# Closing a gated-unit kernel with one barrier: GpSimd waits for the landings between gather and release

## Chip, cores, metric

One core of a Trainium2 chip. The metric is the device time of one execution in microseconds (us). Three runs of the kernel before, taken first, gave a median of 936.13 us (935.86 to 936.99). The program uses one core, so its runs are compared run by run; all runs here are of the fast state, with a granted clock of 1.0.

## The reference

```python
def reference(x):                       # x: 8192 x 8192 float32
    a, b = np.split(x, 2, axis=-1)
    return a * (1 / (1 + np.exp(-b)))   # 8192 x 4096
```

## The kernel before

32 tiles of 128 partitions; each partition holds two rows. SyncE issues loads, ScalarE takes the sigmoid, VectorE multiplies, ScalarE issues stores. The last tile is split in eight pieces, so that its stores start early.

```python
    for i in range(n_tiles):
        x_sb = pool.tile([P, R * n_cols], fp32)
        o_sb = pool.tile([P, R * half], fp32)
        load = nc.sync.dma_start(out=x_sb, in_=x_t[i])
        ...
        n = 4 if i == n_tiles - 1 else 1
        ...                                   # for each row and piece:
                nc.scalar.activation(out=b, in_=b, func=SIG)
                nc.vector.tensor_mul(out=o_sb[:, cols], in0=a, in1=b)
                if n > 1:
                    nc.scalar.dma_start(out=out_t[i, :, cols], in_=o_sb[:, cols])
        if n == 1:
            nc.scalar.dma_start(out=out_t[i], in_=o_sb)
```

The closing is not written in the kernel; the framework adds it as the program's third block. In order: SyncE waits for nine semaphores (eight of DMA lanes, which the transfers use in turn, and one of VectorE) ahead of a drain (an instruction that the traces call DRAIN; it can carry waits and updates of semaphores); barrier one, in which every other engine adds 1 to a gather semaphore and GpSimd, having seen 4, adds 4 to a release semaphore; GpSimd's reset drain and a clear of the kernel's semaphores; barrier two.

## Time and profile before

| | before |
|---|---|
| median of the first 3 runs | 936.13 us |
| span, first to last instruction (profiled run of 935.99 us) | 933.924 us |
| last landing (sixteenth increment of the last store's semaphore) | 933.047 us |
| tail: last landing to the end of the span | 0.877 us |

A store has landed when its semaphore has its sixteenth increment. The page, the queue waits and the closing instructions of this kernel are shown in the prediction. Times to the nanosecond are starts and semaphore updates as the trace records them. "From start to start" is the time from one instruction's start to that of the next one on the path; the durations that the views print are shorter, because waiting and propagation are not in them.

### The profile page before, as it was taken

What the parts mean: (1) busy time and instruction counts of PE and PEld (TensorE: products, weight loads), DVE (VectorE), ACT (ScalarE), POOL (GpSimd) and SP (SyncE); (2) the same over time, 40 slices, a digit from 0 to 9 for tenths busy, and PEclk for the clock granted to TensorE, in tenths of its full rate; (3) what the DMA queues carried; (4) which work ended last, traced back from release to release, by engine and by line L of the source; (5) the groups of instructions that cost most, each with busy time, mean ns of one, the idle gap of its engine ahead of it and who ended that gap; (6) DMA issues with size and microseconds to landing.
All of it is one profiled execution on the core that took longest, in us unless ns stands there. A gap on an engine that the chain in (4) does not pass through costs nothing.

```text
span 933.9 us, 410 instructions
## 1 busy us (share of the span) xinstructions
DVE 280.9 (30%) x70; ACT 230.0 (25%) x71; POOL 0.2 (0%) x4
## 2 busy tenths in 40 slices
DVE  0333321333213333133331333312333123331234
ACT  1313331133311333203332033320233202333023
POOL 0000000000000000000000000000000000000000
DMA  9999999999999999999999999999999999999998
GB/s 404 420 434 431 453 418 429 439 434 449 420 456 404 452 424 427 449 425 451 412 459 410 438 438 425 451 421 452 413 449 421 431 445 443 429 420 453 410 446 362
DMA packets 10226, 402.67 MB, mean 431 GB/s; under 512 B 1136, under 2 KB 1136, under 8 KB 2160
## 3 DMA queue, kind: packets, MB, share of 16 engines
q1 hardware_dynamic: 4608, 268.44, 66.5%
q10 hardware_dynamic: 5616, 134.22, 33.3%
q14 instruction: 2, 0.02, 0.0%
HBM read 268.44 MB, written 134.22 MB: 431 GB/s over the span
## 4 chain that ended last, share of the span: by engine, by line
DMA 78%; DVE 15%; ACT 6%; issue 0%; DVEq 0%; ACTq 0%
DMA x_sb<-in_x_dram 78%; DVE o_sb L39 15%; ACT x_sb L38 6%; DVEq L61 0%; ACTq L41 0%; ACTq L38 0%
## 5 line engine op out<-in xcount | busy, mean ns | idle before, releaser
L39 DVE TENSOR_TENSOR o_sb<-x_sb 128x4096 f32<-128x4096 f32 (+1 forms) x70 | 280.9, 4056 | 647.2 <-ACT x_sb L38 647.2
L38 ACT ACTIVATE x_sb<-x_sb 128x4096 f32<-128x4096 f32 (+1 forms) x70 | 228.7, 3315 | 695.9 <-DMA x_sb<-in_x_dram 691.8
L38 ACT ACT_TABLE_LOAD x1 | 1.3, 1283 | 0.8 <-PEq L85 0.8
L85 POOL MEMSET const-uint8-127<- 128x1 uint8 x1 | 0.1, 103 | 0.0
L85 POOL MEMSET const-bfloat16-1.0<- 128x1 bf16 x1 | 0.1, 102 | 0.0
L85 POOL MEMSET const-float32-0.0<- 128x1 f32 x1 | 0.1, 99 | 0.2 <-issue 0.2
L85 POOL MEMSET const-float32-1.0<- 128x1 f32 x1 | 0.1, 99 | 0.0
## 6 DMA issues: line engine op xcount, KB each, us to landing
out_dram<-o_sb ACTq DMA_DIRECT2D x31, 4096.0 KB, 41.7
out_dram<-o_sb ACTq DMA_DIRECT2D x8, 512.0 KB, 6.2
x_sb<-in_x_dram SPq DMA_DIRECT2D x32, 45.5
```

Of the source, the lines that this page charges most:

```text
L38: nc.scalar.activation(out=b, in_=b, func=SIG)
L39: nc.vector.tensor_mul(out=o_sb[:, cols], in0=a, in1=b)
L85: nc = _bacc.Bacc("TRN2", target_bir_lowering=False, num_devices=1)
```

## The change

The intent: all engines meet once instead of twice. SyncE no longer waits for stores; it arrives early. GpSimd gathers, waits for the landings itself, resets and clears, and then releases.

```diff
-        load = nc.sync.dma_start(out=x_sb, in_=x_t[i])
-        first = first or load
+        nc.sync.dma_start(out=x_sb, in_=x_t[i])
...
+def _launch_early(nc):            # first load ahead of the entry drain, as before
...
+def _one_closing_barrier(nc):
+    block = nc.main_func.blocks[2].instructions
+    waits = block[0]
...
+    drain1, gather1, release1, reset, clear, drain2, gather2, release2 = pool
+    others = [i for i in block[1:] if i.engine != POOL]
+    arrive_and_leave = others[: len(others) // 2]
+    last = stores[-1].sync_info.on_update[0].id
+    landings = sorted(waits.sync_info.on_wait, key=lambda w: w.id == last)
+    pool_waits = [
+        mybir.InstEventSemaphore(engine=POOL, ...on_wait=[w]...)
+        for w in landings
+    ]
+    block[:] = arrive_and_leave + [drain1, gather1, *pool_waits, reset, clear, drain2, release1]
```

More of the change, by code (lines that the diff above doesn't have):

```diff
@@ L22, in _tiles @@
     pool = ctx.enter_context(tc.tile_pool(name="io", bufs=2))
-    first = None
     for i in range(n_tiles):
@@ L43, in _tiles @@
             nc.scalar.dma_start(out=out_t[i], in_=o_sb)
-    return first
+def _launch_early(nc):
+    SP = mybir.EngineType.SP
+    entry, body = (b.instructions for b in nc.main_func.blocks[:2])
+    load = next(i for i in body if i.engine == SP and i.opcode == "DMACopy")
+    assert not load.sync_info.on_wait
+    body.remove(load)
+    where = next(k for k, i in enumerate(entry) if i.engine == SP and i.opcode == "Drain")
+    entry.insert(where, load)
+def _one_closing_barrier(nc):
+    SP, POOL = mybir.EngineType.SP, mybir.EngineType.Pool
+    block = nc.main_func.blocks[2].instructions
+    waits = block[0]
+    assert waits.engine == SP and waits.opcode == "Drain" and len(waits.sync_info.on_wait) > 1
+    pool = [i for i in block if i.engine == POOL]
+    drain1, gather1, release1, reset, clear, drain2, gather2, release2 = pool
+    assert reset.is_reset_sema and clear.opcode == "ISA"
+    others = [i for i in block[1:] if i.engine != POOL]
+    arrive_and_leave = others[: len(others) // 2]
+    stores = [i for i in nc.main_func.blocks[1].instructions if i.opcode == "DMACopy"]
+    last = stores[-1].sync_info.on_update[0].id
+    landings = sorted(waits.sync_info.on_wait, key=lambda w: w.id == last)
+    pool_waits = [
+        mybir.InstEventSemaphore(
+            name=nc.get_next_instruction_name(),
+            engine=POOL,
+            debug=waits.debug,
+            sync_info=mybir.SyncInfo(on_wait=[w], on_update=[]),
+        )
+        for w in landings
+    ]
+    block[:] = arrive_and_leave + [drain1, gather1, *pool_waits, reset, clear, drain2, release1]
 @with_exitstack
@@ L61 @@
     tc.compile()
-    blocks = nc.main_func.blocks
-    entry, body = blocks[0].instructions, blocks[1].instructions
-    SP = mybir.EngineType.SP
-    at = next(k for k, i in enumerate(body) if i.engine == SP)
-    load = body[at]
-    assert load.opcode == "DMACopy" and not load.sync_info.on_wait
-    del body[at]
-    where = next(k for k, i in enumerate(entry) if i.engine == SP and i.opcode == "Drain")
-    entry.insert(where, load)
+    _launch_early(nc)
+    _one_closing_barrier(nc)
 _INS = ['x']
```

## The prediction

> **What bounds the kernel now.** I read the page first, for the limit of the whole run, then the queue waits of SyncE, then narrow windows of the closing line (line 61, to which every closing instruction is booked), and last the semaphore records of the trace for times to the nanosecond. From the page:
>
> ```profile
> span 933.9 us, 410 instructions
> ...
> DVE 280.9 (30%) x70; ACT 230.0 (25%) x71; POOL 0.2 (0%) x4
> ...
> DMA  9999999999999999999999999999999999999998
> ...
> DMA packets 10226, 402.67 MB, mean 431 GB/s; under 512 B 1136, under 2 KB 1136, under 8 KB 2160
> ...
> DMA 78%; DVE 15%; ACT 6%; issue 0%; DVEq 0%; ACTq 0%
> ```
>
> The DMA row is full in every slice but the last; no engine is busy a third of the time. The 402.67 MB set the time. The change moves no byte and no compute instruction, so it can act only after the last transfer has landed. How long is that stretch? SyncE's queue waits name its beginning:
>
> ```profile
> SPq L61 <- DMA out_dram<-o_sb: 63.4, 3, 61.1
> SPq L61 <- PEq L61: 0.6, 2, 0.4
> ```
>
> The first line is SyncE waiting, at the end, for stores to land. The second is SyncE waiting in the barriers, 0.6 us in two waits; nothing of that can be gained beyond what lies after the landing. Windows of 0.25 us at the end (columns: window, its length, busy time of DVE, ACT and POOL, clock, DMA share, GB/s) show the transfers die out:
>
> ```profile
> 932.50:932.75 0.25, 0.00 (x0) 0.00 (x0) 0.00 (x0) 1.00 0.04 16
> 932.75:933.00 0.25, 0.00 (x0) 0.00 (x0) 0.00 (x0) 1.00 0.00 0
> ```
>
> The last packet ends at 932.721 us; the sixteenth increment of the last store's semaphore comes at 933.047. The span ends at 933.924. So everything the change can touch is 933.924 - 933.047 = 0.877 us, 0.09% of the time. GpSimd's closing instructions from 933.3 on (duration in ns, then first and last start):
>
> ```profile
> L61 POOLq EVENT_SEMAPHORE  x3: 17/17/17, 933.4 to 933.8; - x3
> L61 POOLq DRAIN  x2: 34/52/70, 933.4 to 933.7; - x2
> L61 POOLq EVENT_SEMAPHORE_RANGE_CLEAR  x1: 93/93/93, 933.5 to 933.5; - x1
> ```
>
> With the first gather at 933.282 these are: gather, release, reset drain, clear, drain, gather, release. The range clear really is short, 93 ns, so resetting the kernel's semaphores is a small cost; what takes time is the row of steps.
>
> **The 0.877 us, step by step**, each as the time from one start to the next (trace records, ns): landing to SyncE's wait for it, 16; to its next wait instruction (two other semaphores, long satisfied), 64; to the drain that carries the last wait, 68; to the drain that arrives at barrier one, 55; to GpSimd's gather, 32; to its release, 79; to its reset drain, 80; to the clear, 100; to the second drain, 121; to the second gather, 79; to the second release, 78; to the end of the last engine's leaving (TensorE, its 51 ns wait being the slowest), 105. Sum 877. The other engines re-arrive for barrier two by 933.587 us, before GpSimd gathers at 933.741, so the second barrier costs only GpSimd's own instructions.
>
> **What the Trainium skill says.** "Perfetto Trace Analysis", section "Sequencer-only Instruction (DRAIN, etc)": only the execution of such an instruction is reported, the wait before and the propagation after it are not. The trace agrees: the twelve instructions of the path have durations of 28, 28, 7, 7, 17, 17, 70, 93, 34, 17, 17 and 51 ns, 386 together, of 877 from start to start. I therefore count starts, not durations. "DMA: Bandwidth & Descriptors", section "Anatomy of one DMA — SWDGE (gpsimd) path": data move at bytes / 436e9, and the semaphore fires only when the last byte is confirmed in memory. Those transfers are of the software queue and ours of the hardware queues, yet the rate fits: 402.67 MB / 436 GB/s = 923.6 us of the span's 933.9; the confirmation here takes 933.047 - 932.721 = 0.33 us. Neither part is touched. "Runtime: NRT & Kernel Launch", section "The ~15µs preamble/postamble breakdown": a closing barrier of about 1.5 us, a semaphore reset of about 1.5 us and about 2 us of barrier and DMA re-arming follow the kernel. In this case only 935.99 - 933.92 = 2.07 us of the profiled run's time lies outside the span, so not all of that is in the metric; the measurement decides. The changed kernel leaves this part as it is.
>
> **The change part by part.**
> - *Moving the first load ahead of the entry drain* is in both kernels; the diff only rewrites how the load is found. The dropped return value does nothing. 0.
> - *SyncE no longer waits for the landings.* It arrives as soon as its last issue is done. Removed from the path: 16 + 64 + 68 + 55 ns, and the 32 ns from its arrival to the gather: 235 ns.
> - *Gather one moves ahead of the landing.* With SyncE early, the last to arrive is ScalarE, whose closing drain ends at 928.708 us; the gather falls near 928.74, over 4 us before the landing. Its 79 ns to the next instruction leave the path.
> - *GpSimd gets the waits, one semaphore each.* The old waits name nine semaphores in five instructions (four pairs and a single), so nine new instructions. At GpSimd's pace of some 79 ns that is 0.7 us, but the sort puts the last store's semaphore at the end. The store before it lands at 931.813 us, 1.234 us ahead of the last; all eight others are checked by then or at most 8 x 79 = 0.63 us after. One wait is left on the path: from the semaphore's update to GpSimd's start I take 23 ns (in the old gather: 933.259 to 933.282). Added: 23.
> - *Reset, clear and drain stay*, once: 80 from the wait to the reset drain (as from release one to it), 100, 121.
> - *Gather two goes*: 78 ns less. The drain is followed by the one release, 79 ns as a drain was followed by gather two, and the leaving takes 105.
>
> New tail: 23 + 80 + 100 + 121 + 79 + 105 = 508 ns. Removed 235 + 79 + 78 = 392, added 23: gain 369 ns. Check: 877 - 369 = 508. Time: 936.13 - 0.37 = 935.76 us.
>
> **Rivals.**
> - *The nine waits land on the path* (the last store's is not last, or other stores land after it). Then up to eight of 79 ns, 0.63 us, follow the landing and turn the gain into a loss of 0.26: 936.4 us. For it: one wait for each instruction where SyncE took two. Against: the sort, and landings in the order of issue, 1.2 to 1.3 us apart (929.316, 930.575, 931.813, 933.047).
> - *GpSimd is slower than SyncE to see a DMA's semaphore.* The trace has GpSimd waiting only for engines' updates; a poll of 0.1 to 0.2 us would leave 0.2 of gain: 935.9 us.
> - *The gain is hidden outside the span*: if the 2.07 us after and before it are paced by something else, 936.1 us. Against: the trace's first record after the program comes 0.235 us after the last engine leaves, as if it follows it.
> - *Chance.* Three runs of the same kernel range over 935.86 to 936.99, 1.13 us, three times the gain. This is the likeliest to decide the measured sign: a queue that lands a little later outweighs all of this. The result can read as slower without any step being wrong.
> - *More than expected*, because the old barrier disturbs the transfers: I see nothing for it; at the end no engine waits on them and the stretch is 0.09%.
>
> **Range and chances.** The centre is 935.76. The spread of a median of three I take from the old runs, which lie 0.27 under and 0.86 over their median, and make it a little wider for another session: 935.0 to 936.8. To be 2% faster the kernel would have to lose 18.7 us, where the whole tail is 0.877; 2% slower has no source either, only a disturbed run. Within 2%: 0.98.
>
> **What would show it right or wrong.** In the changed kernel's trace: SyncE has no wait for stores at the end; GpSimd's waits start about 928.8 us, all but one before the last landing; one gather and one release; the tail from the sixteenth increment to the span's end is 0.51 us against 0.88. A tail over 0.7 would mean waits on the path or a slow poll; I then look at which wait starts after the landing. If the tail is 0.51 and the time is not lower by 0.37, the transfers or the stretch outside the span took the difference. The landing time itself (933.05) should move only by chance; if it moves in every run by more than 1 us in one direction, my claim that the change acts only after the landing is wrong.

## The result, and the profile after

Six runs each: 935.98 us median after (935.07 to 936.74), 936.02 before (935.64 to 936.99). The ratio is 0.9998, 95% interval 0.9985 to 1.0011: the same. (A ratio is the mean time of one kernel's runs over the mean of the other's of the same rounds, so not quite the ratio of the medians quoted.) By time alone nothing can be said of a gain of 0.37 us.

The page after, with the same rows as before:

```profile
span 934.6 us, 399 instructions
...
DMA  9999999999999999999999999999999999999998
...
DMA packets 10226, 402.67 MB, mean 431 GB/s; under 512 B 1136, under 2 KB 1136, under 8 KB 2160
```

The transfers are the same; 11 instructions are gone. The profiled run is longer than that of before (span 934.628 against 933.924 us), yet its tail is shorter: its last landing is at 934.128 us, 1.08 us later than in the run of before, and the tail is 0.500 us in place of 0.877. SyncE's queue waits show the first part of the change:

```profile
SPq L97 <- PEq L97: 62.7, 1, 62.7
```

All closing instructions are now on line 97. SyncE has one wait there, for the barrier, and none for a store; before, it waited 63.4 us for stores. (The view infers who ended a wait, and names TensorE's queue, PEq. By the semaphore records it is GpSimd's release, at 934.548 us, that SyncE's instruction at 934.565 follows.) GpSimd's closing instructions (duration in ns as minimum, median, maximum, then first and last start in us) show the second part:

```profile
L97 POOLq EVENT_SEMAPHORE  x6: 17/42/43, 931.0 to 934.5; - x6
L97 POOLq DRAIN  x2: 34/52/70, 934.2 to 934.5; - x2
L97 POOLq EVENT_SEMAPHORE_RANGE_CLEAR  x1: 92/92/92, 934.3 to 934.3; - x1
```

Six event instructions: one gather (931.0, three microseconds ahead of the last landing), four waits and one release. The diff writes nine waits. The lowering (the step that makes the program's final instructions) folded them two to an instruction and put the one left over, VectorE's, on the reset drain. The same view cut to the time after the landing (934.13 on) shows what is left on the path:

```profile
L97 POOLq EVENT_SEMAPHORE  x2: 17/30/42, 934.2 to 934.5; - x2
L97 POOLq DRAIN  x2: 34/52/70, 934.2 to 934.5; - x2
...
L97 PEldq EVENT_SEMAPHORE  x1: 51/51/51, 934.6 to 934.6; - x1
```

GpSimd has one wait and one release left here. Before, SyncE had two event instructions and a drain with a wait after the landing, and GpSimd two gathers and two releases. From start to start, in ns:

| step | before | predicted | after |
|---|---|---|---|
| landing to the wait for it | 16 | 23 | 24 |
| SyncE: two more steps, arrival; gather; release | 64+68+55+32+79 | - | - |
| to the reset drain | 80 | 80 | 87 |
| to the clear | 100 | 100 | 99 |
| to the second drain | 121 | 121 | 122 |
| to gather two, to the release | 79+78 | 79 | 63 |
| to the last engine's leaving | 105 | 105 | 105 |
| sum | 877 | 508 | 500 |

### The profile page after: what moved, and what is told of

It reads as the page before. It is cut to its first block, busy times and chain, and to the rows that moved or that the text cites. A ratio compares the mean times of both kernels' runs of the same rounds, so it can differ in the third digit from the quotient of the medians.

```text
span 934.6 us, 399 instructions
## 1 busy us (share of the span) xinstructions
DVE 280.9 (30%) x70; ACT 230.0 (25%) x71; POOL 0.2 (0%) x4
## 4 chain that ended last, share of the span: by engine, by line
DMA 78%; DVE 15%; ACT 6%; issue 0%; DVEq 0%; ACTq 0%
DMA x_sb<-in_x_dram 78%; DVE o_sb L37 15%; ACT x_sb L36 6%; DVEq L97 0%; ACTq L39 0%; ACTq L36 0%
```

## The experiments

In the full kernel the time moves by 1 us from run to run, so most experiments use the kernel cut to its last tile. Its output is wrong: only the last 256 rows are written, and the rest stays as it was found. It takes some 40.5 us. Each tail is read from one trace, so it is that of a single execution. The first four cut kernels ran in one call on one chip, s_last_first, s_release_first and s_no_clear in a second on another, s_last_early in a third; the kernel before, timed in all three, had medians of 935.90, 935.91 and 935.93 us. The cut is this line, and the closing is varied on top of it:

```diff
-    for i in range(n_tiles):
+    for i in range(n_tiles - 1, n_tiles):
```

**The two ends.** The cut kernel with the closing of before, and with that of the change.

> The kernel before cut to its last tile (output wrong on purpose), closing as it was. Theory: the closing after the last landing is the same 0.88 us as in the full kernel (0.877), on a total of 50 to 65 us; run-to-run spread well under the full kernel's 1.1 us, say 0.2, because little is left to vary. Rival (the spread comes from the start or from what lies outside the span): the spread stays near 1 us.

> The changed kernel cut to its last tile (output wrong on purpose). Theory: tail 0.50 us from the sixteenth increment of the last store to the end, so the median is 0.38 us under that of the cut kernel before. Rival one, hidden outside the span: same median within 0.1. Rival two, the gain in time is larger than in the span (the full runs had 1.8 us outside the span against 2.07 in the one run of before that shows it): 0.5 to 0.7 us less.

Measured: tails of 0.791 and 0.499 us; medians of 40.76 us (40.73 to 40.80) and 40.57 us (40.44 to 40.80). In the profiled runs the time falls from 40.73 to 40.44, by as much as the tails; that is partly luck, since the last landing is also 0.047 us earlier (38.109 against 38.156). Over four runs each the medians differ by 0.19, half of the 0.38 expected. By these two alone the gain in device time isn't shown: s_after spreads over 0.36 us, which I had not expected of so short a kernel, and its slowest run is as slow as that of s_before (40.80). The cut kernel's old closing is 0.09 us shorter than the full kernel's, for a reason that SyncE's closing instructions in s_before show:

```profile
L97 SPq EVENT_SEMAPHORE  x6: 17/28/1278, 31.9 to 38.9; - x6
```

One of these waits is recorded with 1278 ns: the one that holds the last store's semaphore (landing at 38.156 us) and the one before it (36.883 us). It stands last in SyncE's row, so only the drain follows; in the full kernel another pair stood between. The record of this wait begins at 36.900 us, 17 ns after the first-named of its two semaphores, and ends just after the second-named. In these traces the order of the names counts, and not which of the two comes first: the three other pairs of SyncE in this trace also begin 17 ns after the first-named, whose second had landed 2.4 us or more before, and they are recorded with 28 ns.

**Half the change: one barrier, SyncE still waits.**

```diff
-    block[:] = arrive_and_leave + [drain1, gather1, *pool_waits, reset, clear, drain2, release1]
+    block[:] = [waits, *arrive_and_leave, drain1, gather1, reset, clear, drain2, release1]
```

> Half of the change, last tile only: one barrier, but SyncE still waits for the landings and arrives after them. Theory: tail 16+64+68+55+32 = 235 ns to the gather, then 80+99+122+63+105: 0.70 us, so 0.17 us less than the cut kernel before. Rival (the second barrier alone is what costs): tail 0.50, as in the changed kernel.

Measured: tail 0.620 us, 0.171 less than s_before; the expected saving of 0.17 is right (the level is lower by the 0.09 just told). Median 40.50 us (40.48 to 40.62), lower than s_after's 40.57 though the tail is 0.121 us longer: the times don't resolve this step. SyncE still holds the long wait, and GpSimd has one gather and one release:

```profile
L97 SPq EVENT_SEMAPHORE  x5: 17/28/1277, 31.8 to 38.6; - x5
L97 POOLq EVENT_SEMAPHORE  x2: 17/17/17, 38.2 to 38.6; - x2
```

**The other half: GpSimd waits, two barriers.**

```diff
-    block[:] = arrive_and_leave + [drain1, gather1, *pool_waits, reset, clear, drain2, release1]
+    arrive_again = others[len(others) // 2 :]
+    block[:] = arrive_and_leave + [drain1, gather1, *pool_waits, release1, reset, clear]
+    block[:] = list(block) + arrive_again + [drain2, gather2, release2]
```

> The other half, last tile only: GpSimd waits for the landings between gather and first release, and the second barrier stays. Theory: tail 24+87+80+99+122+79+78+105 = 0.67 us, 0.20 us less than the cut kernel before. The two halves' gains (0.17 and 0.20) then add up to the whole 0.38. Rival (the move of the waits gains nothing): tail 0.88.

Measured: tail 0.699 us, 0.092 less than s_before, not 0.20. Most of the miss is the shorter level of s_before (0.09 of 0.11); the rest is that the release, which now carries two of the waits, takes 106 ns to the reset drain and not 80. Median 40.58 us (40.55 to 40.73). SyncE waits only in the two barriers, GpSimd has eight event instructions:

```profile
L99 SPq EVENT_SEMAPHORE  x2: 17/17/17, 38.2 to 38.7; - x2
L99 POOLq EVENT_SEMAPHORE  x8: 17/30/43, 35.8 to 38.7; - x8
```

Both halves gain, 0.171 and 0.092 us, 0.263 together, and the whole 0.292. Of the 29 ns missing, 26 are these 106 ns in place of 80: the lowering places the waits differently in each program. The rival "only the second barrier costs" fell with s_one_sync (0.620 against 0.499), and "moving the waits gains nothing" with this run. This is said of the tails, by the traces.

**The order of the waits.** First the sort turned round.

```diff
-    landings = sorted(waits.sync_info.on_wait, key=lambda w: w.id == last)
+    landings = sorted(waits.sync_info.on_wait, key=lambda w: w.id != last)
```

> The changed kernel cut to its last tile, with the one sort key turned round: GpSimd checks the last store's semaphore first, so the others are checked after it has landed. Theory: the waits are folded in pairs, each step costs 87 ns, three to four more steps stand after the landing: tail 0.76 to 0.85 us, against 0.50. Rival (satisfied waits are free, only the last landing counts): tail 0.50 to 0.55.

I had the direction wrong. The tail is 0.412 us, shorter than s_after by 0.087; median 40.27 us (40.22 to 40.29). The trace shows why: the first wait of the list is the one that stays on the reset drain and is checked last, and the pairs are checked ahead of it. The drain starts 24 ns after the landing, and one step of 87 ns is gone. GpSimd's closing in s_last_first: the same six events and two drains as in the changed kernel, the first drain now starting at 38.1 us (landing 38.055, start 38.079):

```profile
L97 POOLq DRAIN  x2: 34/52/70, 38.1 to 38.3; - x2
```

So that run did not test what I meant it for. With the last store's semaphore put into the fifth place instead, the folding checks it first:

```diff
+    pool_waits[4], pool_waits[-1] = pool_waits[-1], pool_waits[4]
     block[:] = arrive_and_leave + [drain1, gather1, *pool_waits, reset, clear, drain2, release1]
```

> The cut changed kernel with the last store's semaphore swapped to the fifth place of the list, which the folding puts into the first pair that GpSimd checks; the other checks then stand after the landing. Theory: each pair costs 87 ns though it is satisfied, so the tail is 24 + 4 x 87 + 99+122+63+105 = 0.76 us, and the time is 0.26 us over the cut changed kernel's 40.5. Rival (satisfied waits are nearly free, only the landing counts): tail 0.50.

Measured: tail 0.728 us, median 40.66 us (40.63 to 40.76). GpSimd's events:

```profile
L98 POOLq EVENT_SEMAPHORE  x6: 17/43/2167, 36.0 to 38.8; - x6
```

The 2167 ns are the first pair, held until the last landing. After it come three pairs and the drain, from start to start 87, 86 and 87 ns, though all their semaphores had been met for over a microsecond. The first of them starts 79 ns after the landing, not 24 + 87 as I had reckoned; that is the 0.03 us under the expected 0.76. Satisfied waits are not free; the rival fell. This is the loss that the prediction's first rival was about (the waits land on the path): 0.23 us over s_after.

**Release ahead of the clear, and no clear at all.**

```diff
-    block[:] = arrive_and_leave + [drain1, gather1, *pool_waits, reset, clear, drain2, release1]
+    block[:] = arrive_and_leave + [drain1, gather1, *pool_waits, release1, reset, clear, drain2]   # s_release_first
+    block[:] = arrive_and_leave + [drain1, gather1, *pool_waits, release1]                         # s_no_clear
```

> The changed kernel cut to its last tile, with the release moved ahead of reset and clear: the other engines leave while GpSimd clears. Theory: tail 24+87+80+99+122+34 = 0.45 us, GpSimd now being the last to end, 0.05 us less than 0.50; hardly to be seen in the time. Rival (what follows starts from the other engines and not from GpSimd): the time falls by 0.25 us or more.

> The changed kernel cut to its last tile, without reset, clear and the drain after them. Theory: tail 24+87+105 = 0.22 us, so 0.28 us less than the cut changed kernel, in span and in time. Rival (the clear only moves to the end of the program, where the same work is done anyway): time within 0.1 of the cut changed kernel. It may also give a wrong result in later rounds if the semaphores are not at zero when it starts again.

s_release_first: tail 0.473 us (0.45 expected, the release again 107 ns for want of 80), median 40.51 us (40.43 to 40.55), against 40.57 for s_after. In the trace the runtime's first record after the program comes 3 ns after the span's end in place of 235: TensorE, the last of the others, had left 232 ns before the end, so it is again 235 ns after the other engines' leaving; but its last comes 2.470 us after the landing, against 2.446 in s_after. By these two traces what follows waits for GpSimd too, and nothing is gained. s_no_clear: tail 0.241 us, 0.258 under s_after, and a median of 40.22 us (40.07 to 40.29), 0.35 lower; GpSimd's closing line holds these events and neither drain nor clear:

```profile
L97 POOLq EVENT_SEMAPHORE  x6: 17/43/43, 35.8 to 38.1; - x6
```

So the clear and its two drains are about half of what is left (0.258 of 0.499). Whether the kernel is still right without the clear can't be read from it, as a cut kernel's output is wrong to begin with; that stays open.

Over the eight cut kernels the times follow the tails only roughly. From the longest tail (0.791) to the shortest (0.241) the median falls by 0.54 us for 0.55 us of tail, and a straight line through the eight rises by 0.9 us for each us of tail; but s_last_first is 0.30 us under s_after for 0.087 of tail, on another chip. A difference of half a microsecond is thus seen in the time; single steps of 0.1 us are seen in the traces alone.

**Does the tail count in the full kernel?** The full kernel before, with 20 more barriers behind its second one.

```diff
+    second = [i for i in block][-11:]      # the 11 instructions of barrier two
+    for _ in range(20):
+        for i in second:
+            kind = mybir.InstDrain if i.opcode == "Drain" else mybir.InstEventSemaphore
+            block.append(kind(name=..., engine=i.engine, debug=i.debug, sync_info=i.sync_info))
```

> The full kernel before with 20 more closing barriers after the second. Theory: a barrier whose slowest engine is TensorE takes from release to release 205 ns to TensorE's next arrival, 21 for its update, 23 to the gather and 79 to the release: 0.33 us, so 20 of them add 6.6 us (0.7%) to span and time, and the tail after the last landing counts one to one in the full kernel. Rival (the tail is partly hidden behind what follows the span): under 5 us.

Measured, with a correct result: 943.13 us median (942.91 to 943.53), ratio 1.0077 (1.0063 to 1.0091), 7.2 us more by the means. The page and GpSimd's closing:

```profile
span 941.1 us, 630 instructions
...
q14 instruction: 5, 0.04, 0.0%
...
L97 POOLq EVENT_SEMAPHORE  x44: 17/17/17, 932.9 to 941.0; - x44
```

Twenty-two gathers and releases in 8.1 us. Of the twenty added periods from release to release, fifteen are 327 or 328 ns, as worked out; two are 362 and 363; three are 588, 665 and 723. The sum is 7.61 us in this trace in place of 6.6. What held the three long ones was not tried, but the trace has a lead: the queue named "instruction" moved five packets in place of two, and the three new ones start at 935.551, 937.199 and 940.946 us, each 0.40 to 0.58 us after the end of one of the long periods (935.148, 936.796, 940.366). So they may go with the fetching of the 220 added instructions. The mean span grows by 7.4 us and the mean time by 7.2; the difference is that of the last column of the next table. The rival, a tail partly hidden behind what follows, fell: time put behind the last landing shows in the time of the full kernel nearly one to one.

**The full kernels once more**, on one chip: the kernel before against itself, the changed kernel, and the changed kernel with the sort turned round (same edit as s_last_first).

> A control: the full kernel before, unchanged, timed against itself. In the runs so far its time lay 2.05 us over its span and that of every other kernel 1.81 to 1.85. Theory (chance and the way a run is taken, not the closing): a ratio of 1.000 within 0.0015, spread 1 us, tail 0.88. If it is a property of this program, its time outside the span is 2.05 again; if it comes from the place in which the kernel before is run, 1.8.

> The changed kernel once more. Theory: tail 0.50 again wherever the last landing falls; landing and time move by 1 us from run to run, so the ratio lies between 0.9985 and 1.0010 and does not resolve a gain of 0.34 us (0.04%). Rival (the change delays the transfers, as its mean span of 934.1 against 933.9 hints): last landing over 933.6 us again and the mean span again over that of before minus 0.38.

> The full changed kernel with the sort turned round, so that the folding puts the last store's semaphore on the reset drain itself. Theory from the cut kernel (tail 0.41 there): tail 24+99+122+63+105 = 0.41 us, 0.09 less than the changed kernel; correct; in the time not to be told from it, ratio to before 0.9985 to 1.0010. Rival (the lowering orders the waits otherwise with other semaphore numbers): tail 0.50 or more.

| run | tail, us | last landing, us | median (range), us | ratio to before (95%) | mean time over span, us |
|---|---|---|---|---|---|
| f_same | 0.877 | 932.685 | 936.06 (935.62 to 936.13) | 1.0001 (0.9987 to 1.0014) | 2.03 |
| f_after_again | 0.500 | 932.885 | 935.21 (934.82 to 936.22) | 0.9993 (0.9981 to 1.0006) | 1.81 |
| f_last_first | 0.414 | 932.758 | 935.44 (935.00 to 936.20) | 0.9995 (0.9983 to 1.0008) | 1.81 |

All three results are correct. The tails repeat to the nanosecond while the landings move: 933.047 and 932.685 for the kernel before, 934.128 and 932.885 for the changed one. The late landing of the first profiled run did not come back, so nothing in the traces speaks for the rival that the change delays transfers. A small delay isn't excluded: eleven runs of the changed kernel have a mean span of 933.86 us, 32 runs of the kernel before 933.93, which is 0.06 less and not 0.38, with a standard error of 0.20. In its own call, against the nine runs of before there, f_after_again's mean span is 0.33 us lower. Both changed kernels come out lower, but each interval includes 1.

The last column is what I cannot explain. In every set of its runs the kernel before takes 2.04 to 2.08 us more than its span (spans are given to 0.1 us, so these are means), its copy 2.03, and all other programs 1.78 to 1.85, the cut kernel with the old closing (1.81) and the one with 20 more barriers (1.81) among them. So it goes with that one program, and not with two barriers or with the place in which it is run. In the device time it favours the changed kernel by another 0.2 us. In the trace itself the other sign shows: the runtime's last record comes 1.901 us after the span's end before and 1.940 after (1.903 in f_same, 1.944 in f_after_again), so 0.04 of the gain is given back there. This does go with the barriers: it is 1.901 to 1.904 in all five traces with two barriers or more, and 1.937 to 1.947 in the eight with one, s_release_first (1.997) left out. From the last landing to the runtime's last record it is 2.778 and 2.780 us before, 2.440 and 2.444 after: 0.34 of the 0.377 us are left at the end of what the trace shows. The causes of both stay open.

The version with the sort turned round has the shortest tail of those that keep the clear, 0.41 against 0.50 and 0.88 us. By the trace it beats both kernels; by the time nothing is shown.

## Why the prediction was right, point by point

- **The time.** 935.76 was named, 935.98 measured, later 935.21: within the range, and the same within 2%. Right, but this says little: the kernel before falls in the same range (936.02, its copy 936.06). The test of the reasoning is the tail.
- **What can change at all.** The tail of 0.877 us was taken as the limit. Right: 0.877 in both traces of that kernel, and f_20_more shows that what stands there counts nearly one to one (7.4 us of span and 7.2 of time on average).
- **The sum.** Tail 508 ns predicted, 500 measured twice. The gain is 0.377 us in the span; 0.369 was predicted. Two terms were off by more than 2 ns: the wait to the reset drain is 87 and not 80, the step after a wait of two semaphores being slower (it is 81 after the one-semaphore gather of s_one_sync), and the second drain to the release 63 and not 79, where I had taken the time to a gather, which waits for a semaphore as the release does not. The two (+7 and -16) partly cancel, so that 500 lies so near to 508 owes something to luck.
- **The clear is a small cost** (93 ns). Misread: the prediction itself counts starts and not durations, and by that count the clear's step is 121 ns; without reset, clear and drain the tail is 0.258 us shorter (s_no_clear).
- **Nine new instructions.** Wrong: four and a share of a drain. It did not matter, because three of the four pairs pass before the last landing. That this was the condition is shown by s_last_early (0.728 us).
- **The sort puts the last landing at the end of the checks.** Not quite: it stands in the last pair, with the drain's wait behind it. f_last_first mends this, 0.086 us.
- **The gather near 928.74 us.** It was at 931.020, because this run's ScalarE ended its closing drain at 930.989; 31 ns lie between, as estimated. Over 4 us ahead became 3. It need not be an effect of the change: ScalarE issues its last store 4.87 us before the last landing in the first trace of before, but 3.65 us in f_same, which is the same kernel, and 3.66 to 3.67 in the three changed full kernels.
- **A slow poll by GpSimd** (second rival). No: 24 ns from a DMA's last increment to GpSimd's start in three changed kernels.
- **Nothing outside the span changes.** This step failed: 0.04 us more in the runtime's own closing, in every trace with one barrier, and 0.2 us less of time over span, for reasons not found. Both are under the spread of the full kernel's times.
- **Chance decides the sign.** Right: the ratio 0.9998 says nothing of 0.37 us, and the profiled run after was the longer one with the shorter tail.

## What to carry to other kernels

Merging two closing barriers and letting the releasing engine wait for the landings saved 0.29 us of tail in a kernel of 40 us (0.7%) and 0.38 in one of 936 (0.04%, invisible in its time). To judge a change far under the run-to-run spread, measure the stretch that it touches in the trace, from the last landing to the end, and cut the kernel so that the rest moves less (here the range of its runs fell from 0.5 to 1.7 us to 0.07 to 0.36). Look in the trace at how waits were really placed: every further instruction with a pair of satisfied waits behind the last landing cost 0.09 us here.

## What the Trainium skill lacked or had wrong

- "Perfetto Trace Analysis", section "Sequencer-only Instruction (DRAIN, etc)", has an instruction start when all its semaphores are satisfied. With two semaphores the record can start when the first-named is satisfied: in s_before a wait is recorded from 36.900 us, with its semaphores met at 36.883 and 38.156 us, for 1278 ns (2167 ns in s_last_early).
- "Runtime: NRT & Kernel Launch", section "The ~15µs preamble/postamble breakdown", lists about 5 us after the kernel (1.5, 1.5 and 2). Here the runtime's last semaphore record comes 1.90 to 1.95 us after the program's last instruction in all the traces with two barriers or one (2.00 with the early release), and the device time lies 1.8 to 2.1 us over the span. What leaves no semaphore record may still follow.
- No page that I read gives the cost of the steps of a program's own closing (what I found is for the runtime's own barriers and resets): 87 ns from start to start for a satisfied wait of two semaphores on GpSimd, 64 ns on SyncE, 328 ns for a whole barrier of five engines as the framework adds it, and about 0.26 us for reset, clear and the drain after them (0.499 less 0.241 us).
